# Expert products of the last 76 keys as three float32r products, with low parts made by GpSimd, and 24 instead of 12 sample slots ahead of the fence

## The chip, the cores and the metric

The kernel runs on one core of a Trainium2 chip. The core has TensorE (matrix products; PE in the profile, with its weight loads as PEld), VectorE (DVE), ScalarE (ACT), GpSimd (POOL) and SyncE (SP). Each engine works through its own queue of instructions in order, and they wait for one another by semaphores. Sixteen DMA engines move data between the memory of the chip and SBUF, the on-chip working memory of 128 partitions. Products are accumulated in PSUM. The metric is the device time of one execution in microseconds; the median of several executions counts.

## The reference

One step of a decoder layer is computed for 512 new prompt tokens and 32 sample tokens (8 sequences of 4), with a width of 1024. A mixer (retention and a convolution module) comes first; what matters here is the expert layer behind it:

```
s1, s2 = q1 . sub_keys_1, q2 . sub_keys_2         # per token and head, 128 keys each
v1, i1 = top16(s1);  v2, i2 = top16(s2)
sv, ci = top16(v1[:, None] + v2[None, :])          # 16 of the 256 sums
idx    = e1 * 128 + e2                             # expert number, 16384 experts
gate   = softmax(sv)
act    = gelu(peer_u[idx] . x)
out    = sum(gate * act * peer_v[idx])             # over 8 heads x 16 experts
```

So every token picks 128 experts. Each expert has a row of 1024 numbers in a first table (`peer_u`) and one in a second table (`peer_v`). All is float32, 544 tokens in all. A layer norm of the residual plus this output ends the step.

## The kernel before

The tokens are treated in two ways. For 288 of them (128 of the prompt, the 32 sample tokens, another 128 of the prompt) the experts' rows are *gathered*: for slot k, one indirect DMA fetches for each of 128 partitions the row pair (first and second table, 8 KB) of one expert, 1 MB in all. For the other 256 tokens (`ND`) the whole tables are read and multiplied densely: 128 *keys* e, each of which stands for 128 experts.

**A gather slot** (`gather`, lines 567 to 586) is: the indirect DMA on GpSimd's queue (L572) into one of the buffers `g`; on VectorE the dot product of the first half with the token, L575, with two inputs in SBUF; on ScalarE the gelu and the gate's scaling, L579 and L580, into `wgt`; on VectorE `acc = v * wgt + acc`, L585, again with two inputs in SBUF. Then the buffer is free. There are three buffers in the pool `gp` and one more in the pool `gx2` that serves every fourth slot of a 128-slot group. The sample tokens (index tile `Is`) lie four to a token over the partitions and have 32 slots; the last group of 128 tokens (`Ib`) has 128.

**The dense part** has for each key e a score step (`scores_of`, L784: load the key's block of the first table into a buffer `uv`, 16 matmul records, then gelu on ScalarE), a gate weight for each token and expert of the key (`build`: ScalarE makes one-hot tiles `off` and `A`, VectorE `M` and `B`, TensorE multiplies them, L875), and the *second-table product* (`v_stage`, L914 to L921): load the key's 128 rows of the second table into a buffer `uv` (512 KB, four such buffers, shared with the score step, loaded on SyncE's queue), and add `weights x rows` in four f32 matmuls, 2 token blocks x 2 halves of the width, into four PSUM accumulators `pB`.

The weights of the keys lie in four tiles: `Gb` (keys 0 to 31), `Gc` (32 to 51), `Ga` (52 to 95) and `Gd` (96 to 127).

**The order.** Scores of the keys in Ga and Gb come first. Then `first_keys` builds the gate weights of the first 96 keys and multiplies them in; its last multiplication is the *fence*: the dot products (L575) of the sample slots from number `FREE` on, and of all slots of the 128-slot group, are ordered behind it on VectorE. After that `run((phases(), 1), (fetched(), 2))` weaves one key's product with two gather slots. `phases` does the products of keys 0 to 31, then of 32 to 95 while `last_keys` builds the weights of the last 32 keys (16 pieces) and afterwards, one per key, the score steps of the last 32 keys run (`s_stage`, with a multiplication L886 on VectorE), and then of 96 to 127. A scheduler that models the run as it builds the program chooses the order of the instructions on each engine within these limits. The kernel ends with two layer norms on the accumulators `pB`.

Of the kernel before, what the change touches and what calls it, by code (L numbers as in the profile page):

```python
# [8 lines left out]
F32 = mybir.dt.float32  # L9
F32R = mybir.dt.float32r  # L10
# [4 lines left out]
AF = mybir.ActivationFunctionType  # L15
# [4 lines left out]
D = 1024  # L20
# [5 lines left out]
PH, NK, TK = 8, 128, 16  # L26
# [5 lines left out]
ND = NR - NG2  # L32
TB = 8
KX = 60
UV = 4
FREE = 12
EG = (32, 20, 44, 32)
E0S = (0, 32, 52, 96)

# [54 lines left out]
def tile_step(ctx: ExitStack, tc: tile.TileContext, a, o):  # L94
    nc = tc.nc
    V, S, T, G = nc.vector, nc.scalar, nc.tensor, nc.gpsimd
# [4 lines left out]
    wps, right = ExitStack(), ExitStack()  # L101
# [32 lines left out]
    def load_w(view, c0, places=(), after=None):  # L134

        ws = []
        for q in range(2):
            w = wp.tile([128, 8, 256], F32, name="w") if not places or places[q] is None else places[q]
            load = nc.sync.dma_start(w, view[c0 // 256 + q])
            if after is not None:  # L140
                behind(load, after)
            ws.append(w)
        return ws

    def load_win(blk):
        return load_w(a["w_in"], blk * 512)
# [18 lines left out]
    def behind(ins, other):  # L165
        tc.add_manual_dep(ins.ins, other.ins.name, mybir.DependencyInfo(
            mybir.DependencyClass.NoSync, mybir.DependencyReason.DATA), reason="order")
# [397 lines left out]
    gx2, fence = [], []  # L565

    def gather(x1, idx, gate, acc, slots):

        for k in slots:
# [5 lines left out]
            dot = V.scalar_tensor_tensor(t[:, :D], t[:, :D], 1.0, x1, op0=OP.mult, op1=OP.mult, accum_out=act[:, 0:1])  # L575
            if fence and (len(slots) == 128 or k >= FREE):
                behind(dot, fence[0])
# [19 lines left out]
    def run(*gens):  # L597

        live = list(gens)
        while live:  # L600
            for g in list(live):
                for _ in range(g[1]):
                    if next(g[0], "end") == "end":
                        live.remove(g)
                        break
# [37 lines left out]
    w = W0[2]  # L643
# [31 lines left out]
    for h0 in range(0, PH, 2):  # L675
        w = load_w(a["w_query"], h0 * 256)
# [18 lines left out]
    w = load_win(2)  # L695
# [75 lines left out]
    GW = {2: gap.tile([128, EG[2], ND], F32, name="Ga")}  # L771

    def place(e):

        g = max(i for i in range(4) if E0S[i] <= e)
        return GW[g][:, e - E0S[g]]

    def scores_of(e):

        u = uvp.tile([128, D], F32, name="uv").rearrange("p (k e) -> p k e", k=8)  # L780
        nc.sync.dma_start(u, a["ut"][e])
        sp = pdn.tile([128, ND], F32, name="sp")
        for k in range(8):
            T.matmul(sp, u[:, k], x1T[:, k, NG2:], start=(k == 0), stop=(k == 7))  # L784
        return sp
# [11 lines left out]
    for h0 in range(0, PH, 2):  # L797
        w = load_w(a["w_query"], h0 * 256)
# [29 lines left out]
    topk_of("s", 0, range(2))  # L828
    for e in range(E0S[2], E0S[3]):
        S.activation(place(e), scores_of(e), AF.Gelu)  # L830
    gbs = ExitStack()
    gb = gbs.enter_context(tc.tile_pool(name="gb", bufs=1, side="right", reuse_waits="tile"))
    GW[0] = gb.tile([128, EG[0], ND], F32, name="Gb")
    for e in range(EG[0]):
        S.activation(place(e), scores_of(e), AF.Gelu)
# [4 lines left out]

    dn = ctx.enter_context(tc.tile_pool(name="dn", bufs=1, reuse_waits="tile"))
    dw_ = ctx.enter_context(tc.tile_pool(name="dw_", bufs=4, reuse_waits="tile"))
    gc = ctx.enter_context(tc.tile_pool(name="gc", bufs=1, reuse_waits="tile"))
    pacc = ctx.enter_context(tc.tile_pool(name="pacc", bufs=1, space=PSUM, reuse_waits="tile"))
    pB = [[pacc.tile([128, 512], F32, name=f"pB{b}{q}") for q in range(2)] for b in range(2)]
    for b in range(2):
# [32 lines left out]
    def s_stage(e, n=ND):  # L879

        sp, G_ = scores_of(e), place(e)
        W = dw_.tile([128, ND], F32, name="W")
        S.activation(W[:, :n], sp[:, :n], AF.Gelu)
        if n < ND:
            S.activation(G_[:, n:], sp[:, n:], AF.Gelu)
        V.tensor_mul(G_[:, :n], G_[:, :n], W[:, :n])  # L886

    def first_keys():

        with tc.tile_pool(name="bt", bufs=2, reuse_waits="tile") as bt:  # L890
            done = 0
            for pt, ts in build(bt, 0, E0S[3], 4):
                for g, e0, e1, ready in ((0, 0, EG[0], True), (2, 0, EG[2], True), (1, 0, done, True), (1, done, EG[1], False)):
                    if e0 == e1:
                        continue
                    to = GW[g][:, e0:e1, ts]
                    part = pt[:, :, E0S[g] + e0:E0S[g] + e1].rearrange("p t e -> p e t")
                    if ready:
                        last = V.tensor_mul(to, to, part)
                    else:  # L900
                        V.tensor_copy(to, part)  # L901
                if ts.stop % 12 == 0 and done < EG[1]:
                    s_stage(E0S[1] + done, ts.stop)
                    done += 1
        return last

    def last_keys():

        with tc.tile_pool(name="bt", bufs=2, reuse_waits="tile") as bt:
            for pt, ts in build(bt, E0S[3], EG[3], 16):  # L910
                S.activation(GW[3][:, :, ts], pt.rearrange("p t e -> p e t"), AF.Copy)
                yield

    def v_stage(e):  # L914
        vt = uvp.tile([128, D], F32, name="uv")
        nc.sync.dma_start(vt, a["uv"][e * NK:(e + 1) * NK, D:])
        W = place(e)
        for b in range(2):
            for q in range(2):
                T.matmul(pB[b][q], W[:, b * 128:(b + 1) * 128], vt[:, q * 512:(q + 1) * 512],  # L920
                         start=False, stop=(e == NK - 1), skip_group_check=True)  # L921

    def phases():
        for e in range(EG[0]):
            v_stage(e)
            yield
        gbs.close()
        gd = ctx.enter_context(tc.tile_pool(name="gd", bufs=1, side="right", reuse_waits="tile"))
        GW[3] = gd.tile([128, EG[3], ND], F32, name="Gd")
        b = last_keys()  # L930
        more = iter(range(E0S[3], NK))
        for e in range(E0S[1], E0S[3]):
            v_stage(e)
            if next(b, "end") == "end":
                for _ in range(1):
                    k = next(more, None)
                    if k is not None:
                        s_stage(k)
            yield
        for e in range(E0S[3], NK):  # L940
            v_stage(e)
            yield

    def fetched():
        t = dn.tile([128, D], F32, name="yt")
        finish(x1_0, [acc0[:, 0:512], acc0[:, 512:]], 128, [(0, 128, o[0][0, 0:128])], t)
        yield
        for g, c0, dst in (("s", 0, o[1].rearrange("b i d -> (b i) d")), ("b", NS, o[0][0, 128:256])):
            w_, r_ = GSP[g]
            x1g = dn.tile([128, D], F32, name="x1g")  # L950
            for b in range(r_):
                nc.scalar.dma_start(x1g[b * w_:(b + 1) * w_], x1_dram[c0:c0 + w_])
            ac = per.tile([128, D], F32, name="acc")
            yield from gather(x1g, Ig[g], GTg[g].rearrange("p h k -> p (h k)"), ac, range(128 // r_))
            t = dn.tile([128, D], F32, name="yt")
            for b in range(1, r_):
                part = dn.tile([128, D], F32, name="yt")
                S.activation(part[:w_], ac[b * w_:(b + 1) * w_], AF.Copy)
                V.tensor_add(ac[:w_], ac[:w_], part[:w_])
            finish(x1g, [ac[:, 0:512], ac[:, 512:]], w_, [(0, w_, dst)], t)  # L960
            yield

    fence.append(first_keys())
    gx2.append(ctx.enter_context(tc.tile_pool(name="gx2", bufs=1, reuse_waits="tile")))
    run((phases(), 1), (fetched(), 2))
    for b in range(2):
        t = uvp.tile([128, D], F32, name="uv")
# [50 lines left out]
```

## Time and profile before

| what | value |
|---|---|
| runs | 1603.92, 1608.52, 1608.15 us; median 1608.15 us |
| profiled execution | 1603.19 us, span of the instructions 1601.4 us |
| TensorE / VectorE / ScalarE / GpSimd busy | 93% / 77% / 38% / 23% of the span |
| mean granted TensorE clock | 0.971 |
| read from memory | 497 MB, 314 GB/s over the span |

The profile is of one execution. Windows give for a stretch (in us from the start of the span) the busy time of each engine with its number of instructions, the granted TensorE clock, the share of time that the 16 DMA engines are busy, and GB/s. A row of the timeline gives start, duration, engine, line, operation, output and inputs, and in brackets the idle time before it with what ended it. A row of a line or a tile gives the number of its instructions, their shortest, median and longest duration in ns, and the first and the last start. The chain of waits is the work that ended last, followed backwards. An f32 matmul leaves two records in the trace, each with a weight load.

### The profile page before, as it was taken

How to read it: one execution, taken by the hardware profiler on the slowest of the kernel's cores; microseconds unless marked ns; L12 is line 12 of the kernel's file. 1: busy time of each engine (PE TensorE's matmuls, PEld its weight loads, DVE VectorE, ACT ScalarE, POOL GpSimd, SP SyncE). 2: the span in 40 equal slices, each digit the busy share in tenths (PEclk: the TensorE clock that was granted, in tenths of full speed). 3: DMA queues.
4: the chain of work that ended last, by engine and by line, in shares of the span. 5: the costliest groups of instructions: out<-in, count | busy, mean ns of one | idle time of the engine just before them, and what ended most of it. 6: DMA issues, size and time to landing. Idle time of an engine off the chain costs nothing.

```text
span 1601.4 us, 20802 instructions
## 1 busy us (share of the span) xinstructions
PE 1494.5 (93%) x7014; PEld 1010.1 (63%) x7014; DVE 1225.3 (77%) x3158; ACT 604.3 (38%) x1687; POOL 374.1 (23%) x335
## 2 busy tenths in 40 slices
PE   6899999996979999999999997999999999999996
PEld 6788556564756667788788875444566655543332
DVE  3939989989865999999852788566777777766666
ACT  2235542254222323333623888413994111111111
POOL 1001423444321222321120000122223222222221
PEclk9899999998989999999999997999999999999998
DMA  9458778997698669997794321998999999999995
GB/s 355 180 195 347 253 280 301 354 364 253 253 383 321 260 250 340 345 340 271 251 413 157 108 86 57 398 402 332 385 365 380 423 424 424 424 423 424 424 424 211
DMA packets 99543, 503.75 MB, mean 315 GB/s; under 512 B 10183, under 2 KB 21191, under 8 KB 56549
## 3 DMA queue, kind: packets, MB, share of 16 engines
q0 software_dynamic: 42240, 305.12, 48.7%
q1 hardware_dynamic: 50749, 189.96, 31.3%
q10 hardware_dynamic: 6448, 7.36, 1.5%
q8 instruction: 55, 0.90, 0.2%
q14 instruction: 51, 0.42, 0.1%
HBM read 497.03 MB, written 5.80 MB: 314 GB/s over the span
## 4 chain that ended last, share of the span: by engine, by line
PE 32%; DMA 28%; DVE 24%; issue 8%; ACT 4%; POOL 2%; SPq 0%; DVEq 0%; POOLq 0%; ACTq 0%
DMA g<-in_uv_dram,Ib 17%; PE pB L920 10%; PE sp L784 9%; PE mm L198 7%; DMA g<-in_uv_dram,I 7%; DVE acc L585 6%; DVE g L575 4%; POOL g L572 2%; ACT off L862 2%; PE mm L875 2%; PE mm L308 2%; DMA g<-in_w_in_dram 2%; DMA uv<-in_uv_dram 1%; DVE iu L504 1%; DVE score L505 1%
## 5 line engine op out<-in xcount | busy, mean ns | idle before, releaser
L784 PE MATMUL sp<-x1T,uv 128*128 128x256 f32 x2048 | 464.7, 384 | 15.4 <-ACT Ga L830 9.4
L784 PEld LDWEIGHTS sp<-x1T,uv 128*128 128x128 f32 x2048 | 385.5, 191 | 89.5 <-issue 23.2
L585 DVE SCALAR_TENSOR_TENSOR acc<-g,wgt,acc 128x1024 f32<-128x1024 f32 x285 | 365.0, 1281 | 99.3 <-ACT wgt L580 98.1
L572 POOL DMA_INDIRECT g<-in_uv_dram,I x128 | 181.9, 1421 | 435.1 <-DVE acc L585 222.6
L579 ACT ACTIVATE act<-act 128x1 f32<-128x1 f32 x288 | 57.9, 201 | 592.4 <-DVE g L575 592.0
L575 DVE SCALAR_TENSOR_TENSOR g<-g,x1g 128x1024 f32<-128x1024 f32 x160 | 195.3, 1224 | 94.2 <-DMA g<-in_uv_dram,Ib 63.1
L572 POOL DMA_INDIRECT g<-in_uv_dram,Ib x128 | 133.5, 1043 | 517.9 <-DVE acc L585 318.5
L575 DVE SCALAR_TENSOR_TENSOR g<-g,x 128x1024 f32<-128x1024 f32 x128 | 155.6, 1217 | 31.9 <-DMA g<-in_uv_dram,I 31.8
L198 PE MATMUL mm<-x1T,w 128*128 128x384 f32 (+1 forms) x512 | 176.1, 500 | 0.2 <-ACT score L524 0.2
L920 PE MATMUL pB<-uv,Ga 128*128 128x512 f32 x352 | 162.1, 604 | 1.1 <-DMA uv<-in_uv_dram 0.8
L862 ACT ACTIVATE off<-row,e1T 128x128 bf16<-128x128 bf16 x512 | 157.8, 388 | 1.5 <-PE mm L875 0.4
L198 PEld LDWEIGHTS mm<-x1T,w 128*128 128x128 f32 x512 | 96.6, 190 | 71.4 <-issue 37.9
L920 PE MATMUL pB<-uv,Gd 128*128 128x512 f32 x256 | 117.2, 601 | 2.1 <-DMA uv<-in_uv_dram 1.0
L920 PE MATMUL pB<-uv,Gb 128*128 128x512 f32 x256 | 115.4, 604 | 2.9 <-DMA uv<-in_uv_dram 2.5
L920 PEld LDWEIGHTS pB<-uv,Ga 128*128 128x128 f32 x352 | 63.7, 189 | 83.7 <-issue 63.1
L920 PEld LDWEIGHTS pB<-uv,Gd 128*128 128x128 f32 x256 | 46.1, 189 | 73.3 <-issue 48.2
L875 PEld LDWEIGHTS <-A 128*128 128x128 bf16 x1536 | 64.6, 100 | 36.6 <-issue 32.0
L920 PEld LDWEIGHTS pB<-uv,Gb 128*128 128x128 f32 x256 | 48.1, 193 | 59.6 <-issue 54.3
L875 PE MATMUL mm<-B,A 128*128 128x96 bf16 (+1 forms) x1536 | 68.4, 197 | 13.3 <-DVE Gc L901 12.4
L864 ACT ACTIVATE A<-off 128x1024 bf16<-128x1024 bf16 x64 | 67.4, 1053 | 28.1 <-PE mm L875 27.7
L870 DVE TENSOR_TENSOR B<-M,gtT 128x768 bf16<-128x768 bf16 (+1 forms) x192 | 69.8, 419 | 9.8 <-PE mm L875 9.6
L920 PE MATMUL pB<-uv,Gc 128*128 128x512 f32 x160 | 72.3, 599 | 0.0
(279 smaller groups left out, 1706.3 us busy)
## 6 DMA issues: line engine op xcount, KB each, us to landing
uv<-in_ut_dram SPq DMA_DIRECT2D x128, 512.0 KB
uv<-in_uv_dram SPq DMA_DIRECT2D x128, 512.0 KB
w<-in_w_in_dram SPq DMA_DIRECT2D x18, 1024.0 KB
w<-in_w_query_dram SPq DMA_DIRECT2D x16, 1024.0 KB
w<-in_w_out_dram SPq DMA_DIRECT2D x7, 1024.0 KB
g<-in_uv_dram,I POOLq DMA_INDIRECT x128, 7.9
keys<-in_state_retention_dram ACTq DMA_DIRECT2D x4, 512.0 KB
out_dram<-keys SPq DMA_DIRECT2D x4, 512.0 KB
```

The source lines that it names most:

```text
L198: T.matmul(p[:, :n], w[m // 2][:, k, (m % 2) * 128:(m % 2 + 1) * 128], xT[:, k, c0:c0 + n], start=(k == 0), stop=(k == 7))
L308: mm = T.matmul(p[:n, q * 256:(q + 1) * 256], xT[:, k, c0:c0 + n], w[q][:, k, :], start=(k == 0), stop=(k == 7))
L572: G.indirect_dma_start(out=t, out_offset=None, in_=a["uv"], in_offset=bass.IndirectOffsetOnAxis(ap=idx[:, k:k + 1], axis=0))
L575: dot = V.scalar_tensor_tensor(t[:, :D], t[:, :D], 1.0, x1, op0=OP.mult, op1=OP.mult, accum_out=act[:, 0:1])
L579: S.activation(act[:, 1:2], act[:, 0:1], AF.Gelu)
L585: V.scalar_tensor_tensor(acc, v, wgt, acc, op0=OP.mult, op1=OP.add)
L784: T.matmul(sp, u[:, k], x1T[:, k, NG2:], start=(k == 0), stop=(k == 7))
L862: S.activation(off[:, t], row, AF.Abs, bias=e1T[:, t1 + t:t1 + t + 1])
L864: S.activation(A, off, AF.Relu, bias=1.0, scale=-1.0)
L870: V.tensor_tensor(B[:, q], M, pairs_of(gtT[:, q], t1).to_broadcast([128, TB // 2, ne, 2]), op=OP.mult)
L875: T.matmul(pt[:, t % nt], A[:, t - t1], B[:, q, (t - t1) // 2, :, t % 2], start=(q == 0), stop=(q == 2))
L920: T.matmul(pB[b][q], W[:, b * 128:(b + 1) * 128], vt[:, q * 512:(q + 1) * 512], start=False, stop=(e == NK - 1), skip_group_check=True)
```

## The change

Four things are changed.

- `FREE` goes from 12 to 24: 24 of the 32 sample slots are no longer ordered behind the fence.
- From key 52 on, `v_stage` splits both factors. ScalarE copies the rows into `vh` and the weights into `Wh`, both of type float32r; GpSimd subtracts these from the originals, which gives the low parts `vl` (128x1024) and `Wl` (128x256). In place of the one f32 product come three float32r products: `Wl x vh`, `Wh x vl` and `Wh x vh`, twelve matmuls a key where there were four. The split tiles lie in a new pool `vhp` with two buffers of each.
- The room for `vhp` is that of `Gc`, whose pool is closed when key 52 is reached. Keys 0 to 51 are multiplied as before.
- So that `Gc`'s pool is the last one opened on its side, `gx2` moves to the other side of SBUF, and `Gd` is no tile of its own any more: the weights of the last 32 keys go into the tile `Gb`, whose first use is over by then (the trace of the changed kernel calls them `Gb`).

```
-FREE = 12
+FREE = 24
...
-    gbs = ExitStack()
-    gb = gbs.enter_context(tc.tile_pool(name="gb", bufs=1, side="right", reuse_waits="tile"))
+    gb = ctx.enter_context(tc.tile_pool(name="gb", bufs=1, side="right", reuse_waits="tile"))
...
-    gc = ctx.enter_context(tc.tile_pool(name="gc", bufs=1, reuse_waits="tile"))
+    gcs = ExitStack()
+    gc = gcs.enter_context(tc.tile_pool(name="gc", bufs=1, reuse_waits="tile"))
...
+    vhp = []
+
     def v_stage(e):
         vt = uvp.tile([128, D], F32, name="uv")
         nc.sync.dma_start(vt, a["uv"][e * NK:(e + 1) * NK, D:])
         W = place(e)
+        if not vhp:
+            terms = ((W, vt),)
+        else:
+            vh, vl = vhp[0].tile([128, D], F32R, name="vh"), vhp[0].tile([128, D], F32R, name="vl")
+            S.activation(vh, vt, AF.Copy)
+            G.tensor_sub(vl, vt, vh.bitcast(F32))
+            Wh, Wl = vhp[0].tile([128, ND], F32R, name="Wh"), vhp[0].tile([128, ND], F32R, name="Wl")
+            S.activation(Wh, W, AF.Copy)
+            G.tensor_sub(Wl, W, Wh.bitcast(F32))
+
+            terms = ((Wl, vh), (Wh, vl), (Wh, vh))
         for b in range(2):
-            for q in range(2):
-                T.matmul(pB[b][q], W[:, b * 128:(b + 1) * 128], vt[:, q * 512:(q + 1) * 512],
-                         start=False, stop=(e == NK - 1), skip_group_check=True)
+            for w, v in terms:
+                for q in range(2):
+                    T.matmul(pB[b][q], w[:, b * 128:(b + 1) * 128], v[:, q * 512:(q + 1) * 512], start=False,
+                             stop=(e == NK - 1 and w is terms[-1][0] and v is terms[-1][1]), skip_group_check=True)
...
-        gbs.close()
-        gd = ctx.enter_context(tc.tile_pool(name="gd", bufs=1, side="right", reuse_waits="tile"))
-        GW[3] = gd.tile([128, EG[3], ND], F32, name="Gd")
+        GW[3] = GW[0]
...
         for e in range(E0S[1], E0S[3]):
+            if e == 52:
+                gcs.close()
+                vhp.append(ctx.enter_context(tc.tile_pool(name="vhp", bufs=2, reuse_waits="tile")))
             v_stage(e)
...
-    gx2.append(ctx.enter_context(tc.tile_pool(name="gx2", bufs=1, reuse_waits="tile")))
+    gx2.append(ctx.enter_context(tc.tile_pool(name="gx2", bufs=1, side="right", reuse_waits="tile")))
```

## The prediction

> **What bounds the kernel now.** I read the page's first part, then the chain of work that ended last, then the windows of the stretch in which the changed products run, then the waits in it.
>
> ```profile
> core 0: 1601.4 us, clock 0.971
> PE 1494.5 (93%) x7014; PEld 1010.1 (63%) x7014; DVE 1225.3 (77%) x3158; ACT 604.3 (38%) x1687; POOL 374.1 (23%) x335
> PE 32%; DMA 28%; DVE 24%; issue 8%; ACT 4%; POOL 2%; SPq 0%; DVEq 0%; POOLq 0%; ACTq 0%
> ```
>
> TensorE is 93% busy, but it holds only 32% of the chain that ended last, nearly level with the transfers. Which stage is whose shows in the windows.
>
> ```profile
> core 0: us, PE busy (x) PEld busy (x) DVE busy (x) ACT busy (x) POOL busy (x), PEclk, DMA share, GB/s
> 834.00:858.00 24.00, 24.00 (x113) 21.13 (x112) 0.38 (x1) 2.68 (x7) 0.94 (x1) 1.00 0.69 263
> 858.00:900.00 42.00, 42.00 (x329) 37.25 (x328) 25.13 (x94) 26.89 (x79) 0.00 (x0) 1.00 0.39 126
> 900.00:960.00 60.00, 55.02 (x521) 47.20 (x520) 49.37 (x187) 53.15 (x150) 0.00 (x0) 0.97 0.27 89
> 960.00:992.00 32.00, 21.28 (x236) 17.13 (x234) 27.09 (x102) 27.62 (x76) 0.00 (x0) 0.73 0.05 17
> 1250.00:1467.00 217.00, 213.76 (x640) 116.37 (x638) 154.18 (x197) 37.30 (x138) 54.08 (x58) 1.00 1.02 424
> 1199.00:1586.00 387.00, 381.43 (x1180) 196.56 (x1178) 273.08 (x355) 74.66 (x270) 97.96 (x100) 1.00 0.99 410
> L920 PE MATMUL pB<-uv,Ga x352: 592/592/697, 1199.5 to 1466.6; 128*128 128x512 f32 x176
> L920 PE MATMUL pB<-uv,Gd x256: 592/592/668, 1467.3 to 1585.9; 128*128 128x512 f32 x128
> ```
>
> The last 76 keys (44 on Ga, 32 on Gd) run from 1199.5 to 1585.9 us. In this stretch TensorE is busy 381 of 387 us and the DMA engines are at 0.99, in its middle at 1.02 and 424 GB/s. Two resources are full at once, so relief of TensorE alone gives little; bytes have to go too. Before 992 us the DMA engines are nearly idle (0.39, 0.27, 0.05). The chain of waits says the same of the stretch:
>
> ```profile
> 1478.40 11.42 DMA g<-in_uv_dram,Ib
> 1491.68 1.30 DVE acc L585
> 1493.23 11.46 DMA g<-in_uv_dram,Ib
> POOL g L572 <- DVE acc L585: 270.8, 98, 6.2
> ```
>
> A gather lands 11.4 us after its issue, VectorE works on it, its buffer comes free, the next gather is issued: 14.8 us a round over four buffers. GpSimd stands 271 us in front of gathers, waiting for VectorE. That idle time is what the change means to fill.
>
> **TensorE's part.** A key's four f32 products give way to twelve float32r ones.
>
> ```profile
> 1084.43 27.73 PE pB L920 x64
> 1307.22 3.69 PE L784 MATMUL sp<-x1T,uv 128*128 128x256 f32 x16
> 976.58 2.08 PE L875 MATMUL mm<-B,A 128*128 128x96 bf16 x24 [2.21 <-DVE Gc L901]
> ```
>
> An f32 product of 512 columns leaves two records of 27.73/64 = 0.433 us, 0.87 us in all, a key 3.47 us. No float32r row exists. Ceiling: the f32 price, 12 x 0.87 = 10.4 us a key. Floor: the bf16 issue, 2.08/24 = 0.087 us, 1.05 us a key. I take one record per product, as the 16-bit matmuls leave: between 1.05 and 12 x 0.433 = 5.2 us a key. Both stay under the 6.2 us a key that comes out below, so this term does not set the end; the f32 price would, and is a rival. The Trainium skill, "FP8 and Floating Point Precision", TensorE Precision Notes, has true FP32 as four passes and a reduced-precision form that truncates to FP22; were that one pass, a key would take about 2.6 us, an estimate from the page, and the sum would be the same.
>
> **The 12 slots ahead of the fence.** Twelve gathers with their 24 VectorE instructions leave the late stretch for the time before 992 us. In the order as built, five of the twelve pairs stand before the first L899, seven in the first third of the building of the weights.
>
> ```profile
> 829.14 1.29 DVE L585 SCALAR_TENSOR_TENSOR acc<-g,wgt,acc 128x1024 f32<-128x1024 f32 x1 [0.60 <-ACT wgt L580]
> 833.09 1.28 DVE L585 SCALAR_TENSOR_TENSOR acc<-g,wgt,acc 128x1024 f32<-128x1024 f32 x1 [0.60 <-ACT wgt L580]
> 858.73 0.29 DVE L899 TENSOR_TENSOR Gb<-Gb,mm 128x128 f32<-128x128 f32 x1 [24.36 <-ACT Gb L835]
> ```
>
> Slots come 3.95 us apart, so five need 20 us and fit into the 24.4 us for which VectorE is idle. Seven pairs of 2.5 us are 18 us against slack of 42.0 - 25.1 = 17 us up to 900 and 60 - 49.4 = 11 us up to 960: between 0 and 18 us, and I take +5, since the slack there is mostly large enough but comes in pieces behind TensorE. The 24 activations are a few tenths each in 107 of 134 us busy. What the 12 save later: 12 x 1.049 MB, 29.7 us at 424 GB/s, or 30 us of VectorE. GpSimd's queue has nothing else to do before the fence.
>
> **ScalarE.** Each of the 76 keys gets two copies, vh of the row length and Wh of 256.
>
> ```profile
> L583 ACT ACTIVATE acc<-g,wgt x3: 1134/1149/1152, 139.1 to 1093.9; 128x1024 f32<-128x1024 f32 x3
> L835 ACT ACTIVATE Gb<-sp x32: 358/383/385, 744.3 to 858.3; 128x256 f32<-128x256 f32 x32
> ```
>
> 76 x (1.15 + 0.38) = 116 us beside 75 us in 387: hidden, and still hidden if both cost double. But vh waits for its row to land, and behind it in ScalarE's queue stand the two small activations of a gather, for which L585 waits, and behind that the next gather. With four row buffers the row is asked for early, so I cost this wait at nothing; uncovered, it is at most a few us a key.
>
> **GpSimd's part, which decides.** Per key one subtraction of 128x1024 and one of 128x256. They stand in one queue with the gathers, each of which waits for its buffer. Row buffers now come free when vl is made, not when TensorE is done, and so the row loads and score loads on SyncE's queue follow GpSimd's pace. No row shows a subtraction on GpSimd; these are near:
>
> ```profile
> 1588.18 1.22 DVE L454 TENSOR_TENSOR yt<-yt,lng 128x1024 f32<-128x1024 f32 x1
> 1588.13 0.14 DVE L451 SCALAR_TENSOR_TENSOR lrs<-lmv,lrs 128x1 f32<-128x1 f32 x1
> 1585.74 0.23 POOL L183 TENSOR_SCALAR lrs<-lmv 128x1 f32<-128x1 f32 x1 [17.42 <-DVE lmv L448]
> 2.56 0.09 POOL L179 MEMSET eps_c<- 128x1 f32 x1
> 2.58 0.19 POOL L190 MEMSET u_p<- 128x120 f32 x1
> L886 DVE TENSOR_TENSOR Gd<-Gd,W x32: 410/421/476, 1221.1 to 1408.8; 128x256 f32<-128x256 f32 x32
> ```
>
> Floor: VectorE's prices, 1.22 + 0.42 = 1.64 us a key. Ceiling: GpSimd's memset streams 0.84 ns an element (0.10 us for 119); three streams one after the other, two in and one out, are 2.7 + 0.7 = 3.4 us. I take VectorE's prices times 0.23/0.14 = 1.64, the ratio of the two engines' smallest operations: 2.0 + 0.69 = 2.7 us a key, 204 us for 76. The Trainium skill, "GPSIMD Engine Reference", Elementwise side-by-side cycle accounting, has an f32 add of 2048 at 4497 ns; half of that is 2.25 us for vl, an estimate, and about 2.8 us a key, 9 us more on the sum. No run here shows it.
>
> Whether these 204 us fit into GpSimd's idle time hangs on what VectorE does meanwhile:
>
> ```profile
> 389.67 1.28 DVE L585 SCALAR_TENSOR_TENSOR acc<-g,wgt,acc 128x1024 f32<-128x1024 f32 x1
> 389.92 1.12 POOL L183 TENSOR_SCALAR hrs<-hrs 128x4 f32<-128x4 f32 x1 [4.12 <-ACT act L579]
> 391.12 1.04 POOL L184 TENSOR_TENSOR hrs<-hrs,mhalf 128x4 f32<-128x4 f32 x1
> 391.42 1.23 DVE L575 SCALAR_TENSOR_TENSOR g<-g,x 128x1024 f32<-128x1024 f32 x1 [0.46 <-DMA g<-in_uv_dram,I]
> 1587.44 0.57 POOL L184 TENSOR_TENSOR lrs<-lrs,mhalf 128x1 f32<-128x1 f32 x1
> 1589.99 1.22 DVE L455 TENSOR_TENSOR yt<-yt,lnb 128x1024 f32<-128x1024 f32 x1
> 1590.24 1.40 POOL L184 TENSOR_TENSOR lrs<-lrs,mhalf 128x1 f32<-128x1 f32 x1
> ```
>
> A GpSimd instruction of 0.23 us that began inside L585 took 1.12 us and ended at 391.04, 0.09 us after L585. One of 0.57 us that began inside L455 took 1.40 us and ended 0.43 us after it. Both VectorE instructions read two tensors in SBUF; it looks as if GpSimd's reads are held until such an instruction is over. The other way round the rows are silent: L575 at 391.42 kept its 1.23 us beside a GpSimd operation of four elements, too small to tell. The Trainium skill, "SBUF — State Buffer", Who interferes with whom, has a rule for it: VectorE with two SBUF inputs and GpSimd reading SBUF share one read port, and whoever starts first keeps it for the whole instruction. In the direction that the rows show, the trace agrees; by the page L575 and L585 would be held behind vl as well, which no row here shows.
>
> In either direction the times add, since the two kinds of work never overlap. L575 and L585, the gather's two instructions, are both of the two-input kind, and so is L886:
>
> ```profile
> L585 DVE SCALAR_TENSOR_TENSOR acc<-g,wgt,acc x103: 1276/1285/1287, 1201.5 to 1581.6; 128x1024 f32<-128x1024 f32 x103
> L575 DVE SCALAR_TENSOR_TENSOR g<-g,x1g x102: 1212/1225/1233, 1198.4 to 1579.8; 128x1024 f32<-128x1024 f32 x102
> L572 POOL DMA_INDIRECT g<-in_uv_dram,Ib x99: 932/932/1907, 1203.1 to 1567.4; - x99
> ```
>
> Of 102 pairs 12 are gone: 90 x (1.225 + 1.285) = 226 us, L886 32 x 0.42 = 13, GpSimd 204: 443 us. Between the two halves of a pair lie 0.60 us in which VectorE has nothing to read; a subtraction can use such a gap only if GpSimd doesn't stand before a gather then. None to all of 90 x 0.60 = 54 us may be lost; I take half, 27. That makes 470 us, 6.2 us a key, where it was 387 before.
>
> **The sum.** 1199.3 + 5 (fence) + 470 + 3 (the last key's products) + 15.4 (1601.4 - 1586.0, the closing norms, unchanged) = 1693 us of span, 91 more than 1601.4. The profiled execution took 1603.2 us, so 1695 us; the median of the runs lies 5 us above that execution, so against the median it is 5.4% more rather than 5.7%.
>
> **Rivals.** *GpSimd's work hides, and it gets faster.* Speaking for it: 271 us of GpSimd idle, and one-sided rows. Then the stretch is bound by bytes: 410 GB/s x 387 us = 158.7 MB, less 12.6, is 146.1 MB, 345 us at 424; GpSimd needs 204 + 87 x 0.93 = 285, TensorE 32 x 3.69 = 118 for the scores and 76 keys at 1.05 to 5.2 = 80 to 395 us, 198 to 513 in all, so this rival also wants a float32r key under 3.2 us. In the built order 13 keys' vl stand behind the last gather: their 13 x 0.52 = 6.8 MB (16 us) leave the byte-bound part and 13 x 2.7 = 35 us follow: 364 us. Span 1199.3 + 5 + 364 + 3 + 15.4 = 1587, time 1589, 0.9% faster. Against it: the two held instructions. It decides at 1.8 us a key: (387 - 8 - 239)/76. Under exclusion GpSimd must make both low parts in less than that for the kernel not to be slower; the floor of 1.64 lies below it. Chance 0.16.
>
> *Level.* Exclusion with subtractions of about 1.8 us and every gap used: 1600 to 1612 us, chance 0.06.
>
> *float32r at the f32 price.* 76 x 10.4 + 118 = 908 us of TensorE in the stretch, time about 2133. For it: no row of the type. Against: the product has no use then. Chance 0.05. With two records and a stretch of 513 us the time would be about 1738, inside the range.
>
> **How the numbers follow.** Exclusion with a price above the break-even has 0.73, and 1695 is its time. Its own range: without lost gaps 1668, with vl and Wl at the ceiling (258 us) and all gaps 1776; with subtractions of 2.1 us a key and no gaps 1624. So 1625 to 1760 for eight in ten. The full range takes in the faster rival, 1582, and reaches 1755. Faster by over 0.3% 0.16, within 0.3% 0.06, slower 0.78; 0.3% is about what a measurement of this kernel can tell from no change.
>
> **What would show it.** Right: in the stretch of the last 76 keys L575 and L585 average well over 1.23 and 1.29 us or vl and Wl well over 2.0 and 0.7, the DMA share falls from 0.99 to about 0.8, TensorE waits for vl or Wl, and the key's pace is near 6 us. The fence moves by 0 to 18 us, and about 90 pairs stand behind 1199 us. Wrong: DMA share still at 1.0 with plain durations (the faster rival); matmul records that fill the stretch (float32r); a TensorE whose granted clock falls in the gaps, for which no row of this stretch gives a price; ScalarE's small activations late behind vh.

## The result, and the profile after

On the same chip the changed kernel took 1744.78 us (median, 1741.32 to 1748.04) and the kernel before 1606.04 us (1601.45 to 1608.52): a ratio of 1.087, with a 95% interval of 1.0846 to 1.0894. It is 139 us slower. The prediction had the sign and the mechanism; its 1695 us is 50 us too low, inside its range of 1582 to 1755.

The span with the granted clock, the busy times, and four windows of the late stretch of the changed kernel (columns as before: busy time with the number of records, granted TensorE clock, DMA share, GB/s):

```profile
core 0: 1745.9 us, clock 0.930
PE 1496.8 (86%) x7318; PEld 1105.1 (63%) x7318; DVE 1375.4 (79%) x3158; ACT 700.9 (40%) x1839; POOL 703.4 (40%) x487
1300.00:1400.00 100.00, 72.76 (x290) 57.07 (x288) 80.43 (x78) 29.53 (x77) 76.20 (x44) 0.93 0.92 335
1500.00:1600.00 100.00, 67.74 (x220) 49.29 (x218) 76.31 (x48) 32.56 (x70) 91.33 (x52) 0.83 0.74 254
1600.00:1700.00 100.00, 67.31 (x220) 48.68 (x220) 81.04 (x45) 30.21 (x64) 89.82 (x49) 0.83 0.63 220
1700.00:1746.00 46.00, 25.73 (x92) 18.74 (x92) 14.64 (x23) 12.21 (x17) 24.89 (x21) 0.82 0.22 80
```

TensorE was 99% busy in the last 76 keys and the DMA engines were at 0.99. Now neither is full: TensorE falls to 73 and then 67 of 100 us and the DMA share to 0.92, 0.74, 0.63. Two engines look busy in their place, VectorE and GpSimd. Their busy time, though, holds waiting that the record counts as work. The rows of the stretch by line (count, shortest, median and longest duration in ns, first and last start):

```profile
L585 DVE SCALAR_TENSOR_TENSOR acc<-g,wgt,acc x91: 1272/1437/6262, 1200.1 to 1693.5; 128x1024 f32<-128x1024 f32 x91
L575 DVE SCALAR_TENSOR_TENSOR g<-g,x1g x89: 1210/1221/6397, 1203.7 to 1690.3; 128x1024 f32<-128x1024 f32 x89
L927 POOL TENSOR_TENSOR vl<-uv,vh x76: 2333/2368/2817, 1211.7 to 1727.6; 128x1024 fp32r<-128x1024 f32 x76
L930 POOL TENSOR_TENSOR Wl<-Ga,Wh x44: 724/1588/1781, 1207.4 to 1561.5; 128x256 fp32r<-128x256 f32 x44
L930 POOL TENSOR_TENSOR Wl<-Gb,Wh x32: 714/1709/1787, 1567.5 to 1729.9; 128x256 fp32r<-128x256 f32 x32
L572 POOL DMA_INDIRECT g<-in_uv_dram,Ib x87: 935/1697/1992, 1201.7 to 1670.0; - x87
L936 PE MATMUL pB<-vh,Wl x304: 387/397/797, 1213.7 to 1732.4; 128*128 128x512 f32 x152
```

The gather's second VectorE instruction, at most 1.287 us before, now takes up to 6.26 us; the small subtraction takes 0.71 to 1.79 us for one and the same shape. What stands beside them at such times is in the timeline (start, duration, engine, line; in brackets the idle time before and what ended it):

```profile
1298.84 1.44 DVE L585 SCALAR_TENSOR_TENSOR acc<-g,wgt,acc 128x1024 f32<-128x1024 f32 x1 [0.60 <-ACT wgt L580]
1299.09 1.77 POOL L930 TENSOR_TENSOR Wl<-Ga,Wh 128x256 fp32r<-128x256 f32 x1
...
1303.75 1.22 DVE L575 SCALAR_TENSOR_TENSOR g<-g,x1g 128x1024 f32<-128x1024 f32 x1
1304.11 1.68 POOL L572 DMA_INDIRECT g<-in_uv_dram,Ib  x1 [1.33 <-DVE acc L585]
...
1305.58 3.67 DVE L585 SCALAR_TENSOR_TENSOR acc<-g,wgt,acc 128x1024 f32<-128x1024 f32 x1 [0.26 <-ACT wgt L580]
1305.80 2.36 POOL L927 TENSOR_TENSOR vl<-uv,vh 128x1024 fp32r<-128x1024 f32 x1
...
1313.55 0.73 POOL L930 TENSOR_TENSOR Wl<-Ga,Wh 128x256 fp32r<-128x256 f32 x1
```

- At 1305.58 L585 starts 0.22 us ahead of vl, while the gather issue of 1304.11 still runs. vl keeps its 2.36 us and ends at 1308.16; L585 ends 1.09 us later. VectorE is the one that was held. The trace of the kernel before had no row for this direction.
- At 1298.84 the same L585 comes first, and Wl, which needs 0.73 us when nothing stands beside it (1313.55), takes 1.77 and ends 0.58 us after L585. GpSimd was held.
- At 1304.11 the issue of a gather that starts inside L575 takes 1.68 us. Issues beside nothing take 0.935.

That is the exclusion of the prediction, now in both directions. The Trainium skill, "SBUF — State Buffer", Who interferes with whom, says that a VectorE instruction with both inputs in SBUF contends with a GpSimd instruction that reads SBUF; the trace agrees, with 3.67 against 1.28 us and 1.77 against 0.73.

The waits of the stretch from 1200 to 1730 us (who waited for whom: total us, times, longest):

```profile
ACT Wh L929 <- PE pB L936: 91.0, 33, 7.0
POOL g L572 <- DVE acc L585: 84.0, 44, 5.0
DVE acc L585 <- ACT wgt L580: 77.9, 79, 5.6
PE pB L936 <- POOL Wl L930: 64.5, 24, 5.0
PE pB L936 <- POOL vl L927: 42.5, 25, 4.3
```

GpSimd's 271 us of waiting before gathers have shrunk to 84, TensorE waits 107 us for low parts, and L585 waits 78 us for the gate's scaling (79 waits), where it waited 54 before (97 waits).

### The profile page after: what moved, and what is told of

It reads as the page before. It is cut to its first block, busy times and chain, and to the rows that moved or that the text cites. A ratio compares the mean times of both kernels' runs of the same rounds, so it can differ in the third digit from the quotient of the medians.

```text
span 1745.9 us, 21849 instructions
## 1 busy us (share of the span) xinstructions
PE 1496.8 (86%) x7318; PEld 1105.1 (63%) x7318; DVE 1375.4 (79%) x3158; ACT 700.9 (40%) x1839; POOL 703.4 (40%) x487
## 5 line engine op out<-in xcount | busy, mean ns | idle before, releaser
L585 DVE SCALAR_TENSOR_TENSOR acc<-g,wgt,acc 128x1024 f32<-128x1024 f32 x285 | 452.6, 1588 | 140.4 <-ACT wgt L580 139.4
L572 POOL DMA_INDIRECT g<-in_uv_dram,Ib x128 | 184.1, 1438 | 298.4 <-DVE acc L585 162.6
L575 DVE SCALAR_TENSOR_TENSOR g<-g,x1g 128x1024 f32<-128x1024 f32 x160 | 238.9, 1496 | 35.2 <-DMA g<-in_uv_dram,Is 19.9
L936 PE MATMUL pB<-vh,Wl 128*128 128x512 f32 x304 | 109.5, 468 | 100.5 <-POOL Wl L930 65.8
L927 POOL TENSOR_TENSOR vl<-uv,vh 128x1024 fp32r<-128x1024 f32 x76 | 181.9, 2396 | 18.2 <-ACT vh L926 14.6
L575 DVE SCALAR_TENSOR_TENSOR g<-g,x 128x1024 f32<-128x1024 f32 x128 | 155.5, 1216 | 33.0 <-DMA g<-in_uv_dram,I 32.6
L936 PE MATMUL pB<-vl,Wh 128*128 128x512 f32 x304 | 116.9, 471 | 42.5 <-POOL vl L927 42.5
L936 PEld LDWEIGHTS pB<-vh,Wl 128*128 128x128 f32 x304 | 62.9, 220 | 130.5 <-POOL Wl L930 79.0
L936 PE MATMUL pB<-vh,Wh 128*128 128x512 f32 x304 | 112.5, 457 | 0.0
L936 PEld LDWEIGHTS pB<-vl,Wh 128*128 128x128 f32 x304 | 66.1, 226 | 67.9 <-POOL vl L927 53.8
L926 ACT ACTIVATE vh<-uv 128x1024 fp32r<-128x1024 f32 x76 | 79.5, 1048 | 64.4 <-PE pB L936 39.4
```

The costliest lines, as they stand in the source:

```text
L572: G.indirect_dma_start(out=t, out_offset=None, in_=a["uv"], in_offset=bass.IndirectOffsetOnAxis(ap=idx[:, k:k + 1], axis=0))
L585: V.scalar_tensor_tensor(acc, v, wgt, acc, op0=OP.mult, op1=OP.add)
L926: S.activation(vh, vt, AF.Copy)
L927: G.tensor_sub(vl, vt, vh.bitcast(F32))
L936: T.matmul(pB[b][q], w[:, b * 128:(b + 1) * 128], v[:, q * 512:(q + 1) * 512], start=False, stop=(e == NK - 1 and w is terms[-1][0] and v ...
```

## The experiments

Three theories were set against one another. *Exclusion*: the subtractions on GpSimd and the gather's two VectorE instructions cannot run together, so their times add. *Queue*: the low parts merely stand in one queue with the gathers, and each delays the other. *Coupling*: the split itself, its copies and the waits that it adds on ScalarE, spoils the stretch whatever engine subtracts. The kernel before, run beside them, had medians of 1605.41 (e1 to e4), 1603.38 (e5 to e8) and 1602.81 us (e9 to e12); ratios are to those.

### The 24 slots alone, and the split alone

e1 is the kernel before with one line changed:

```
-FREE = 12
+FREE = 24
```

> The kernel before with 24 instead of 12 sample slots ahead of the fence, nothing else. Exclusion theory (VectorE instructions with two SBUF inputs and GpSimd instructions that read SBUF never overlap): it says nothing against this part; in the last stretch TensorE needs 76 x 3.47 + 32 x 3.69 = 382 of 387 us, so with 12.6 MB less to fetch TensorE alone is the bound there, and the fence comes 5 to 10 us later: 1600 to 1612 us, level with before. Bytes theory (the transfers alone set the end of the kernel before): 30 us less minus the fence's delay, 1580 to 1588 us.

It took 1598.65 us, ratio 0.9974 [0.9954, 0.9994]. The time lies just under the band of the theory that calls TensorE the bound, and 11 us over the other. Its windows from 1400 us:

```profile
1400.00:1500.00 100.00, 99.34 (x233) 41.85 (x232) 69.32 (x85) 14.51 (x58) 26.75 (x27) 1.00 1.02 423
1500.00:1600.00 100.00, 86.63 (x198) 36.58 (x196) 34.88 (x49) 8.31 (x22) 7.06 (x11) 0.94 0.54 207
```

Until 1500 us both are still full. The last L585 starts at 1529.8 us, the DMA share falls to 0.54, and TensorE goes on with f32 products to 1586.3, where the kernel before began its last at 1585.9. With 12 gathers fewer there, the bytes are through early and TensorE alone sets the end. Before the fence the slots cost nothing that can be seen: the last L899 starts at 985.0 us, at 992.1 in the kernel before, and between 981 and 996 in the profiles of e2 to e8.

e2 is the changed kernel with the other half undone:

```
-FREE = 24
+FREE = 12
```

> The changed kernel with 12 sample slots ahead of the fence, as before the change. Exclusion theory: twelve more pairs of VectorE instructions, 12 x 2.5 = 30 us, and twelve more gather issues must share with the subtractions, less some 8 us of earlier fence: 1765 to 1790 us. Queue theory (GpSimd's own busy time and the order of its queue set the pace, whatever the instructions read): 12 gather issues of 1.7 us = 20 us, less 8: 1750 to 1760 us.

It took 1789.69 us, 1.1149 [1.1114, 1.1183]: 45 us over the changed kernel. Twelve pairs of 2.51 us are 30 us if they only add. So the slots, worth 0.3% alone, are worth more than their VectorE time beside the split, as the exclusion's upper figure had it. The queue theory's 1750 to 1760 us was missed by 30. The split alone costs 11%.

### The subtractions on VectorE

```
-            G.tensor_sub(vl, vt, vh.bitcast(F32))
+            V.tensor_sub(vl, vt, vh.bitcast(F32))
...
-            G.tensor_sub(Wl, W, Wh.bitcast(F32))
+            V.tensor_sub(Wl, W, Wh.bitcast(F32))
```

> The changed kernel with both low parts made by VectorE instead of GpSimd. Exclusion theory and queue theory alike: no GpSimd subtraction is left; VectorE has 90 x 2.51 + 13 + 76 x 1.64 = 364 us of work in the last stretch, TensorE about 316, the transfers 345: a stretch of 370 to 400 us and 1595 to 1630 us. Coupling theory (the loss lies in the float32r products, in TensorE's lower granted clock or in ScalarE's queue, where vh stands in front of the gathers' activations): little changes, over 1690 us.

It took 1611.06 us, 1.0043 [1.0015, 1.0071]: 134 us of the 139 are gone, with copies, pools and twelve products a key unchanged. Coupling, which forecast over 1690 us, falls as the main cause. Exclusion and queue both allow this. VectorE does 93.52 us of work in 100 there:

```profile
1400.00:1500.00 100.00, 85.78 (x344) 66.01 (x343) 93.52 (x124) 44.75 (x101) 39.96 (x24) 0.95 1.00 396
```

### GpSimd just as busy, without reading

GpSimd writes zeros instead of subtracting, with as many elements as fill about the same time (the low parts are thereby left out of the sum):

```
-            G.tensor_sub(vl, vt, vh.bitcast(F32))
+            for c in (D, D, D // 2):
+                G.memset(vl[:, :c].bitcast(F32), 0.0)
...
-            G.tensor_sub(Wl, W, Wh.bitcast(F32))
+            for _ in range(2):
+                G.memset(Wl.bitcast(F32), 0.0)
```

> The changed kernel with each GpSimd subtraction replaced by GpSimd fills of zero into the same low-part tiles (two and a half row lengths for vl, two of 256 for Wl, about 2.4 and 0.6 us by the memset's 0.84 ns an element); so the low parts are left out of the products, and the fills do not wait for the high parts. GpSimd's queue is as long as before in time and order, but it only writes. Exclusion theory: L575 and L585 go back to 1.23 and 1.29 us and the kernel to 1590 to 1630 us. Queue theory: 1710 to 1745 us, GpSimd's busy time in the stretch as long as in the changed kernel. If the fills exclude VectorE too, L585 keeps its mean of well over 1.4 us and the time stays as well.

It took 1613.79 us, 1.0063 [1.0036, 1.0091]. A window and two rows of the late stretch:

```profile
1400.00:1500.00 100.00, 77.42 (x320) 58.19 (x319) 51.34 (x64) 41.77 (x95) 94.06 (x145) 1.00 0.96 358
L585 DVE SCALAR_TENSOR_TENSOR acc<-g,wgt,acc x88: 1280/1285/1287, 1206.5 to 1590.6; 128x1024 f32<-128x1024 f32 x88
L572 POOL DMA_INDIRECT g<-in_uv_dram,Ib x86: 934/944/2016, 1199.4 to 1581.7; - x86
```

GpSimd is busier there than in the changed kernel in the same window, 94 against 68 of 100 us, with its work in the same queue, and not one L585 is longer than 1.287 us. So it isn't the length of the queue that stretches the gather's instructions but that GpSimd reads. Two things besides the reading differ. The scheduler chose the order anew: behind the last gather stand 13 of the 76 `vl` in the changed kernel and a single fill here. And the fills don't wait for `vh` and `Wh`. So the time alone would not decide between the theories; the durations do, and the copies below, which do not wait for `vh` and `Wh` either, stretch L585 again. The Trainium skill, "SBUF — State Buffer", Who interferes with whom, says that a VectorE instruction with two SBUF inputs does not contend with a GpSimd instruction that only writes SBUF; the trace agrees, with 1.287 us at the longest.

### No low parts at all

Only the product of the two high parts stays; the low parts are left out:

```
-            terms = ((Wl, vh), (Wh, vl), (Wh, vh))
+            terms = ((Wh, vh),)
```

(with the two subtractions and their tiles gone).

> The changed kernel with the product Wh x vh alone in the last 76 keys: the low parts and the two products with them are left out, so GpSimd subtracts nothing and the output lacks their share. TensorE then needs 76 x 0.9 + 118 = 186 us in the stretch, VectorE 239. Bytes theory (with TensorE relieved, the 146 MB of the stretch at 424 GB/s = 345 us set the end): 1570 to 1582 us. Coupling theory (vh and Wh wait in ScalarE's queue for their buffers, and the gathers' small activations stand behind them): the wait of L585 for wgt stays over 100 us, as it was 135 us with the fills, against 47 us in the kernel before with 24 slots, and the time lies at 1595 to 1620 us.

It took 1576.29 us, 0.9843 [0.9806, 0.988]. Its windows:

```profile
1300.00:1400.00 100.00, 74.39 (x287) 55.42 (x285) 69.13 (x94) 37.00 (x97) 38.22 (x26) 0.95 1.02 420
1400.00:1500.00 100.00, 57.47 (x120) 34.12 (x120) 55.45 (x69) 50.80 (x108) 38.85 (x23) 0.55 1.01 408
```

The DMA engines are full until 1500 us while TensorE idles: bytes set the pace, as the bytes theory had it with 1570 to 1582 us. Coupling's time of 1595 to 1620 falls again, though the wait that it named is there: L585 waited 104 us for `wgt`, against 52 us in e1. So that wait alone does not set the time. Without the low parts and without the two products that they need, the changed kernel would have gained 1.6%.

### Only the large subtraction on VectorE

```
-            G.tensor_sub(vl, vt, vh.bitcast(F32))
+            V.tensor_sub(vl, vt, vh.bitcast(F32))
```

> The changed kernel with vl made by VectorE and only Wl left to GpSimd. Exclusion theory: the times add, VectorE 226 + 13 + 76 x 1.22 = 332 us, GpSimd 76 x 0.73 = 55 us, 387 us and 27 to 54 us of gaps: 1640 to 1670 us, and Wl takes 1.5 us or more in the mean where it needs 0.73. Hidden: 55 us of GpSimd vanish in its idle time and the kernel is as the one with both low parts on VectorE, 1603 to 1620 us.

It took 1624.16 us, 1.0151 [1.0114, 1.0188]: between the two forecasts, so a miss for both. The small subtraction on GpSimd costs 13 us over e3 (by the two ratios 17), where VectorE does both, while 76 x 0.73 = 55 us of it ran there:

```profile
L930 POOL TENSOR_TENSOR Wl<-Ga,Wh x44: 725/1314/1807, 1198.6 to 1488.8; 128x256 fp32r<-128x256 f32 x44
L930 POOL TENSOR_TENSOR Wl<-Gb,Wh x32: 736/892/1843, 1492.7 to 1598.9; 128x256 fp32r<-128x256 f32 x32
```

Here GpSimd is mostly the one that is held (medians 1.31 and 0.89 for 0.73; the mean over all 76 is 1.19, where exclusion had 1.5 or more), and no L585 exceeds 1.76 us. For pieces of 0.7 us the whole sum was too much. That they slip mostly into the 0.60 us between the halves of a pair fits the numbers, but was only argued.

### GpSimd reading with one input

Each subtraction becomes two copies of one input, so `vl` and `Wl` hold the whole rows and weights and not the low parts:

```
-            G.tensor_sub(vl, vt, vh.bitcast(F32))
+            for _ in range(2):
+                G.tensor_copy(vl, vt)
...
-            G.tensor_sub(Wl, W, Wh.bitcast(F32))
+            for _ in range(2):
+                G.tensor_copy(Wl, W)
```

> The changed kernel with each GpSimd subtraction replaced by two GpSimd copies of one operand each (the rows into vl twice, the weights into Wl twice); the low parts are then wrong, and the copies do not wait for the high parts. One SBUF input in place of two, about the GpSimd time of the fills. Exclusion by any GpSimd read: about 2.5 us a key as for the fills, 226 + 13 + 190 = 429 us and 27 to 54 us of gaps: 1680 to 1715 us, with L585 and L575 far over 1.29 and 1.23 us at the longest. If only a GpSimd instruction with two inputs excludes VectorE: like the fills, 1605 to 1625 us.

It took 1773.95 us, 1.1075 [1.1028, 1.1122]. The durations answer the question, the time does not:

```profile
L585 DVE SCALAR_TENSOR_TENSOR acc<-g,wgt,acc x91: 1273/1368/3678, 1199.6 to 1599.3; 128x1024 f32<-128x1024 f32 x91
L928 POOL CAST vl<-uv x152: 1027/1044/2030, 1210.8 to 1755.8; 128x1024 fp32r<-128x1024 f32 x152
L932 POOL CAST Wl<-Ga x88: 386/564/1460, 1206.0 to 1639.2; 128x256 fp32r<-128x256 f32 x88
...
1253.12 3.65 DVE L585 SCALAR_TENSOR_TENSOR acc<-g,wgt,acc 128x1024 f32<-128x1024 f32 x1 [0.60 <-ACT wgt L580]
1254.66 1.03 POOL L928 CAST vl<-uv 128x1024 fp32r<-128x1024 f32 x1
```

The L585 of 1253.12 is held while three copies pass; the row shown is the last of them, and L585 ends 1.08 us after it. L585 is held to 3.68 us and the copies to 2.03 and 1.46, so one input on GpSimd's side is enough. But the time is 59 us above the band. The gathers are over at 1600 us, and 41 of the 76 keys then go on alone to 1756: the order of the work is another, gathers ahead of keys, and the keys' remainder was left without cover. What this order costs by itself was not separated.

### The split for half of the keys

e3 with the split for the odd keys from 53 to 95 and the last 32 only:

```
-        if not vhp:
+        if not vhp or (e < E0S[3] and e % 2 == 0):
```

> The kernel with both low parts on VectorE, but with three products only for every second key from 53 to 95 and for the last 32 keys, 54 in all; the other 22 stay single f32 products. VectorE 226 + 13 + 54 x 1.64 = 328 us, TensorE 22 x 3.47 + 54 x 2.6 + 118 = 335, transfers 345: if these three overlap, 1570 to 1590 us, faster than before. Coupling theory: 1595 to 1610 us, as with all 76 keys on VectorE.

It took 1600.74 us, 0.999 [0.9968, 1.0012]: level with the kernel before, where 1570 to 1590 was expected of an overlap that works. The number of the coupling theory, 1595 to 1610, came. From 1300 to 1500 us the DMA engines are still full, at 1.02 and 0.99, with TensorE at 92 and 85 of 100 us and VectorE at 79 and 83; what keeps the rest from overlapping was not separated. So coupling, which falls as the cause of the 139 us, stays open as the reason why the relief of TensorE does not pay even with VectorE subtracting.

### The split where no gathers are left

e1 left 16 keys after the last gather to TensorE alone. Four versions of the changed kernel split only the last keys, 16 (112 in the edit) or 32 (96):

```
-        if not vhp:
+        if not vhp or e < 112:
```

e9 and e11 have the subtractions on VectorE, as in e3; e10 and e12 leave them on GpSimd.

> The changed kernel, split for the last 16 keys only (112 to 127), both subtractions by VectorE; the other keys stay single f32 products. With 24 slots free alone the gathers were done at 1530 us and 16 to 17 keys followed at TensorE's pace, 3.47 us each, with VectorE idle. A split key needs 12 x 0.215 = 2.6 us of TensorE, 1.64 us of VectorE, 1.46 us of ScalarE. If TensorE is the bound there, as that run showed, 16 x 0.87 = 14 us go: 1585 us (1580 to 1590). If a split key cannot keep TensorE's pace because copy, subtraction and product follow one another over two buffers, as in the run with the split of 54 keys, about 3.4 us a key and level with 1599.

> The changed kernel, split for the last 16 keys only, both subtractions on GpSimd. Exclusion theory: VectorE has no gathers left there, so nothing is held; GpSimd's own pace is 2.36 + 0.73 = 3.09 us a key against 3.47 us for the f32 product: 16 x 0.38 = 6 us go, 1592 us (1587 to 1598), and L585 stays at 1.28 us in all but the last few. If the subtraction on GpSimd costs because of itself or its queue and not because of what it stands beside: above 1605.

> The changed kernel, split for the last 32 keys only (96 to 127), by VectorE. Twice the relief of TensorE, 32 x 0.87 = 28 us, but 16 of the keys now stand beside gathers, where the DMA engines are at 0.96 to 1.02 and VectorE is two thirds busy. If those keys gain as well: 1571 us (1565 to 1580). If bytes set the pace until the gathers are done, only the last 16 gain: 1582 to 1592. If the keys beside gathers cost more than they give: level with 1599.

> The changed kernel, split for the last 32 keys only, both subtractions on GpSimd. Exclusion theory: from 1472 us, where these keys begin, some 16 pairs of 2.51 us are left (40 us) and 32 x 3.09 = 99 us of GpSimd cannot run beside them: 1472 + 139 + 5 of lost gaps = 1616, and 15 for the end, 1630 us (1612 to 1640). If GpSimd's work ran beside the gathers, its 99 us would end at 1571 and the time would be 1586 to 1600.

| kernel | keys split, by | time, us | ratio |
|---|---|---|---|
| e9 | last 16, VectorE | 1594.81 | 0.9953 [0.993, 0.9975] |
| e10 | last 16, GpSimd | 1610.97 | 1.0051 [1.0029, 1.0073] |
| e11 | last 32, VectorE | 1595.22 | 0.9948 [0.9923, 0.9972] |
| e12 | last 32, GpSimd | 1646.27 | 1.0255 [1.022, 1.029] |

e12 is the sharpest of them. It adds 16 keys to e10 that stand beside gathers, and 35 us; e11 adds the same 16 keys on VectorE to e9, and nothing. Rows of e12 in that part:

```profile
1554.32 7.11 DVE L575 SCALAR_TENSOR_TENSOR g<-g,x1g 128x1024 f32<-128x1024 f32 x1
1554.94 4.72 POOL L927 TENSOR_TENSOR vl<-uv,vh 128x1024 fp32r<-128x1024 f32 x2
1559.63 0.71 POOL L930 TENSOR_TENSOR Wl<-Gb,Wh 128x256 fp32r<-128x256 f32 x1
```

One L575 is held for 7.11 us while two vl and one Wl pass. The 1646 us of e12 lie over the 1612 to 1640 that the sum gave, and far from the 1586 to 1600 of work that overlaps.

e10 missed: 1592 was forecast and the number of its rival, over 1605, came. No gather stands beside its keys, and no L585 is longer than 1.287 us. But the closing layer norm of the gathered tokens stands beside the first keys, and VectorE's instructions of two inputs in it are held. The row of e10, and the same one of e1, where GpSimd subtracts nothing:

```profile
1527.68 5.55 DVE L592 SCALAR_TENSOR_TENSOR yt<-x1g,acc 128x512 f32<-128x512 f32 x2
...
1531.15 1.29 DVE L592 SCALAR_TENSOR_TENSOR yt<-x1g,acc 128x512 f32<-128x512 f32 x2
```

So exclusion has a part in e10 that its forecast left out. From 1543.8 us on no such instruction is left, and something else sets the pace. The chain of waits repeats with this period (start, duration, what):

```profile
1551.89 0.29 POOL vl L927
1552.18 2.08 issue
1554.26 0.74 POOL Wl L930
...
1555.04 1.25 PE pB L936 x5
...
1558.14 1.07 ACT vh L926
...
1559.28 0.29 POOL vl L927
```

From one vl to the next of this chain are 7.39 us, for two keys: 3.7 us a key, where 3.09 was forecast and the f32 product takes 3.47. Subtraction, product and the next copy follow one another in it; with two tiles of each kind a copy waits for a product to free one (the products begun at 1555.04 end at 1558.05, the copy starts at 1558.14). All sixteen keys took 65.6 us, from 1526.1 to 1591.7, where f32 products at 3.47 us a key take 55.5. That is 10 us more, of the 12 us by which the median of e10 lies over that of e1. On VectorE the same chain is shorter. e9's last keys, in its chain:

```profile
1549.41 5.74 PE pB L936 x24
```

24 products, two keys, in 5.74 us: 2.87 us a key at TensorE's own pace, and this goes on for the last 13 keys. But the first three keys took until 1543.65 from 1530.9, 4.2 us each, beside the layer norm of the gathered tokens on VectorE and ScalarE. So e9 gained about 4 us on e1's time and not 14, between its two forecasts and a miss for both. e11's median, 1595, lies between its cases, a miss as well. e9 and e11 are the best full-precision versions run, half a per cent under the kernel before; their intervals overlap with that of e1, so the split's own gain there is not established.

## Why the prediction came out as it did

**The bound before: right, but sharper than written.** "Relief of TensorE alone gives little; bytes have to go too": e1 shows that with the bytes of 12 gathers gone TensorE sets the end, and e5 that with TensorE relieved the DMA engines stay full until 1500 us and the time is 1576.

**The exclusion: right, in both directions.** L575 averages 1.72 us and L585 2.27 us in the stretch (groups by line, 88 and 89 instructions) against 1.225 and 1.285; the DMA share fell as foretold; e4 against the changed kernel separates reads from queue length, and e3 and e12 put the loss where GpSimd subtracts beside the gathers. The rival that all hides falls with it, and so does the level one. Two of the signs that the prediction listed against itself showed too, without being the cause: ScalarE's small activations came later (L585 waited 78 us for them), but in e4 that wait was 138 us at 1614 us; and TensorE's granted clock fell to 0.83, with TensorE idle for a third of the time.

**float32r: right.** One record per product: 304 for four products of each of 76 keys, and no pair of records. A key takes 2.87 us where nothing holds TensorE up (e9), inside the 1.05 to 5.2 that were taken. It doesn't set the end in the changed kernel. The rival at the f32 price falls.

**The 12 slots: nearly right in size, not in place.** The fence itself stands at 992.9 us against 992.1, so the 5 us that the prediction gave it did not come. Yet the first subtraction starts at 1207.4 us (the row of Wl), where the sum had 1204.3 for the start, 3 us more than taken. Where these 8 us arise behind the fence was not looked for; the first Wl of e6 starts at 1198.6. About 90 pairs stood behind 1199 us, as foretold.

**GpSimd's price: mis-sized.** Taken 2.0 + 0.69 = 2.7 us a key; measured without company 2.36 + 0.73 = 3.09, inside the floor and ceiling of 1.64 and 3.4. Over 76 keys 235 us rather than 204: +31 us of the miss. The Trainium skill, "GPSIMD Engine Reference", Elementwise side-by-side cycle accounting, would have given an estimate of 2.25 us for vl, half of its 4497 ns; the measured 2.36 agrees within 5%, and the prediction had the better number beside it and took the worse.

**The lost gaps: mis-sized.** 226 + 13 + 235 = 474 us of work that excludes itself. The stretch from 1207 to the end of the last Wl at 1730.7 is 524, so 50 us were lost where 27 were taken (up to 54 was the bound): +23. The 50 are what the other terms leave over. Two places are seen for it. The prediction costed ScalarE's wait at nothing and looked at vh; the wait is at Wh, which stands 91 us in all for TensorE to free its buffer, and behind it the gather's small activations, for which L585 waited 78 rather than 54 us. That this cost time is not shown: in e4 both waits are longer, 144.5 and 138.2 us. And after the last L585, begun at 1693.5, nine keys remained, 37 us at 4.1 us each instead of 3.09. At first the closing layer norm of the gathered tokens stands beside them and excludes (L592 takes 3.89 us for 1.29). Behind it the chain shows the copy again standing behind a subtraction:

```profile
1725.65 0.75 POOL Wl L930
1726.40 0.05 issue
1726.45 1.07 ACT vh L926
1727.52 0.07 issue
1727.59 2.39 POOL vl L927
1729.97 0.69 POOL Wl L930
```

**The sum.** +3 from the start, +31 from the price, +23 from the gaps are 57, less 3 because the last products and the closing norms took 15.2 us (1730.7 to 1745.9) where 3 + 15.4 were taken: 1692.7 + 54 = 1747 against the profiled span of 1745.9. Since the gaps are the remainder, that this comes out is no test of them. (The profiled execution took 1747.7 us, 3 us over the median.) The break-even of 1.8 us a key left the lost gaps out: e3 has 1.64 us a key and came out 0.4% slower and not level. With the 27 us of gaps the same sum gives 1199.3 + 5 + (226 + 13 + 125 + 27) + 3 + 15.4 = 1614 us of span for e3, whose profiled span is 1601.7 and whose median time 1611. How much of the 50 us belongs to the gather's longer issue, 1.70 for 0.93 us, was not separated; in e3 the issues are as long (median 1.68) without such a loss.

**The range.** The prediction gave 1625 to 1760 us for eight cases in ten and 1755 us as the upper end of the whole; the two don't fit together, since the narrower band reaches higher. The measured 1745 us lies in both, near the upper end.

## What to carry to other kernels

An idle engine is only free capacity if its work uses nothing that a busy engine holds: GpSimd waited 271 us here, and 235 us of subtractions put into that time went with a loss of 139, of which 134 are gone when VectorE subtracts, because they read SBUF beside VectorE instructions with two inputs. Look first at what the busy engine's instructions read, and for one row in which the two overlap. Where they exclude each other, add their times for long pieces; short pieces cost less than the sum here (e6). Put a piece where the other engine is idle, and count layer norms and the like among its work (e10). Work that is made in three engines one after the other also wants enough buffers, or its sum of latencies becomes the pace, as 3.7 us a key for 3.09 us of work.

## What the runs showed of the hardware that was not expected

- The issue of an indirect gather on GpSimd is held by a two-input VectorE instruction too: 1.68 us when it starts inside L575 against 0.935, and it ends 0.82 us after L575 does (1304.97 and 1305.79). Between 1200 and 1590 us of the kernel before, 91 issues start outside such an instruction and take 0.93 or 0.94 us; in e3, where GpSimd does little else, 83 of 86 start inside one, and their median is 1.68.
- One input on GpSimd's side is enough to exclude (e7), and writing alone is not (e4).
- An instruction held once can be passed by several of the other engine: 7.11 us for L575 in e12.
- TensorE's granted clock fell to 0.83 in the changed kernel's last windows with TensorE 67% busy, and to 0.55 in e5 at 57%. What that costs was not measured apart; in e5 the bytes set the pace anyway.
